# Two transformer blocks on one core: another order at the start of the mixers, fewer splits on GpSimd, and a shifted side job in the first feed-forward layer

## The chip, the cores and the metric

The kernel runs on one core of a Trainium2 chip. The metric is the device time of one execution in microseconds (us); the kernel before has three such runs, and beside them one execution was profiled. The engines are named as in the profile: PE (TensorE, matmuls; PEld its weight loads), DVE (VectorE), ACT (ScalarE), POOL (GpSimd) and SP (SyncE, which here issues nearly all DMAs; SPq is its queue). Each engine runs its own list of instructions strictly in order.

## The reference, cut to what matters

```
def first_block(x, c, ...):                 # x (1, 256, 1024), two layers
    cond = silu(c)
    for l in range(2):
        mod = cond @ ada_w[l] + ada_b[l]    # nine vectors of 1024: shift, scale, gate of three sublayers
        h = rms_norm(x, norm_g[l, 0]) * (1 + scale0) + shift0
        x = x + 0.5 * gate0 * swiglu(h, ffn1_w13[l], ffn1_w2[l])       # "ffn1"
        h = rms_norm(x, norm_g[l, 1]) * (1 + scale1) + shift1
        p = split(h @ w_in[l] + b_in[l])
        y = concat(nsa(p.a, t5 bias tables), short_conv(p.b), gated_deltanet(causal_conv4(p.c)), mlstm(p.d))
        x = x + gate1 * (y @ w_out[l])                                  # "mixer"
        x = x + 0.5 * gate2 * swiglu(adaln(x), ffn2_w13[l], ffn2_w2[l]) # "ffn2"
    return x
# second_block: LRU and latent attention, MLP, retention, MLP; the change does not touch it
```

All is float32. A product is made of three matmuls on rounded parts: each operand is split into `hi` (rounded) and `lo` (the rest), and hi·hi, hi·lo and lo·hi are summed in PSUM.

## The kernel before, in words

**Weights.** All weights lie in one HBM stream in the order of their use. `weights(key)` loads a chunk (128 partitions x 1024, 896 or 768 floats, 0.5 MB for 1024) with one DMA on the SP queue into a buffer `wraw` (4 buffers, L140); ACT copies it to `whi` (L150) and DVE, or POOL where the call passes `True`, subtracts to get `wlo` (L151). `whi` and `wlo` have 4 buffers each, so the loads can run 8 chunks ahead of PE. A 1024 chunk feeds 24 matmuls of 256 to 258 columns (L167, L168, L169).

**Order.** A scheduler that works with a timing model puts the instructions of each engine in order, from the program text and the priorities in it. `issue_after(last(SP))` ties a DMA to the one before it; while `in_order` is set (all of ffn1 of layer 0 up to w2) the SP queue keeps the order of the program text.

**ffn1 of layer 0** takes 0 to 245 us. The function `begin` does the first feature tiles (m = 0 to 7) with the normalisation still open, because the conditioning vectors `mod` are still being computed: a conditioning step loads a 0.5 MB chunk of `ada_w` into `wada` (3 buffers), multiplies it with `cond` and sums on DVE (L233, "a conditioning pass"). Of the 32 passes that go with this layer's scale, gate and shift vectors, `next(more)` in `begin` calls 4, the loop over m = 8 to 21 one per m, and the loop of the second product (w2, eight output tiles m with three chunks each) up to two per m. `begin` also computes `shift0` on PE by thin matmuls ("strips"), whose weights go through `wada` too. The loop over m ends each m with the gate: DVE multiplies by `rstd` (L384), ACT applies silu, DVE forms `sb` (L392), ACT and POOL split it into `g`.

**The side job** builds the relative-position bias tables. From m = SIDE = 12 on, each m calls `next(sides)` once: the loads of `ident`, `cst`, `tab` and `onehot` and four matmuls `st<-onehot,tab` (L474) with four copies `bv<-st` on ACT (L475) come first, then at the next m the store of `bv` to a DRAM scratch `bdram` (L484, on the SP queue), two m later the skewed load `bt<-bdram` (L487), and later the copies to `bc` (L494).

**A mixer** (layer 0: 245 to 456 us, layer 1: 846 to 1060 us) begins with six products of the gated-deltanet inputs (chunks `wc`, on un-normalised input) and one of scalars (`wsc`), all with their `wlo` split on POOL. `inputs()` then evacuates them: for each of six tiles DVE multiplies PSUM by `rstd` (`cxp`, L591) and adds a bias column (`cb`, L592), ACT adds the bias (L593), and DVE does the four taps of the causal convolution (`cx`, L595 and three times L597) with a sigmoid gate (L603). In its midst `scalars()` (L699 to L707) makes `scT` on DVE and transposes it on PE (L705). `norm()` makes the normed input `h` for the other products: `nt` (L349, DVE), `hhi` (L352, ACT), `hlo` (L353, DVE), eight tiles of each. Then come the product of `wa_3`, the token-major product `wta` in `proj_tok` (L733 to L735), the compression (L1180 on), and the rest. `weave` interleaves these generators by the numbers in `PACE`.

## Time and profile before

| | us |
|---|---|
| runs (three) | 1990.77, 1995.83, 1999.63; median 1995.83 |
| profiled execution, its own time | 2000.48 |
| its span in the trace | 1998.6 |
| PE busy in the span | 1926.8 |
| DVE, ACT, POOL busy | 1501.9, 1009.7, 566.0 |

Times in the trace count from the span's start. PEclk is the granted TensorE clock as a share of full speed; over the whole span it is 0.975. An instruction's duration overlaps the next one's a little on DVE, so starts lie closer than durations.

### The profile page before, as it was taken

The numbers are of one execution on the slowest core, as the hardware profiler recorded it, in microseconds if no ns is written. First come the engines' busy times: TensorE is split into PE (matmuls) and PEld (weight loads), VectorE is DVE, ScalarE is ACT, GpSimd is POOL, SyncE is SP. The second block draws the span as 40 slices with busy tenths as digits, with TensorE's granted clock in tenths as the row PEclk, the third lists the DMA queues.
The fourth block names the chain that finished last, engine by engine and source line by source line (L and its number), as shares of the span: only waits on it lengthen the run. The fifth ranks groups of instructions, "written<-read, shape, count | busy, mean of one in ns | idle before, by whom it ended". The sixth has DMA issues, their size and how long they took to land.

```text
span 1998.6 us, 40143 instructions
## 1 busy us (share of the span) xinstructions
PE 1926.8 (96%) x16031; PEld 1827.9 (91%) x16031; DVE 1501.9 (75%) x2693; ACT 1009.7 (51%) x1712; POOL 566.0 (28%) x474
## 2 busy tenths in 40 slices
...
GB/s 332 271 218 316 209 131 261 109 87 240 286 279 259 264 287 280 304 142 176 63 35 210 221 189 194 142 80 136 159 190 166 194 131 156 150 158 195 174 202 95
DMA packets 108808, 384.21 MB, mean 192 GB/s; under 512 B 12075, under 2 KB 14668, under 8 KB 108364
## 3 DMA queue, kind: packets, MB, share of 16 engines
...
## 4 chain that ended last, share of the span: by engine, by line
PE 85%; DVE 7%; DMA 3%; issue 2%; ACT 1%; POOL 1%; SPq 0%; POOLq 0%; ACTq 0%; DVEq 0%
PE acc L167 23%; PE acc L169 23%; PE acc L168 23%; DMA wraw<-in_stream_dram 2%; DVE wlo L151 1%; PE b L2007 1%; DVE wada L233 1%; PE pa L1284 1%; ACT whi L150 1%; PE pc L924 1%; PE pa L1311 1%; DVE vlo L292 1%; DMA g<-in_stream_dram 1%; PE pc L942 1%; PE acc L733 1%
## 5 line engine op out<-in xcount | busy, mean ns | idle before, releaser
L150 ACT ACTIVATE whi<-wraw 128x1024 fp32r<-128x1024 f32 (+2 forms) x546 | 563.5, 1036 | 466.3 <-PE acc L168 323.9
L151 DVE TENSOR_TENSOR wlo<-wraw,whi 128x1024 fp32r<-128x1024 f32 (+1 forms) x471 | 594.9, 1266 | 204.1 <-ACT whi L150 197.5
L167 PE MATMUL acc<-vhi,whi 128*128 128x258 f32 (+3 forms) x2176 | 621.7, 288 | 21.2 <-ACT whi L150 17.6
L168 PE MATMUL acc<-vlo,whi 128*128 128x258 f32 (+3 forms) x2176 | 620.8, 286 | 2.4 <-DVE vlo L292 2.4
L169 PE MATMUL acc<-vhi,wlo 128*128 128x258 f32 (+3 forms) x2176 | 615.6, 286 | 3.1 <-DVE wlo L151 3.0
L167 PEld LDWEIGHTS acc<-vhi,whi 128*128 128x128 f32 x2176 | 413.1, 191 | 28.9 <-ACT whi L150 19.5
L168 PEld LDWEIGHTS acc<-vlo,whi 128*128 128x128 f32 x2176 | 416.0, 191 | 5.3 <-DVE vlo L292 3.2
L169 PEld LDWEIGHTS acc<-vhi,wlo 128*128 128x128 f32 x2176 | 411.6, 190 | 6.9 <-DVE wlo L151 4.0
L151 POOL TENSOR_TENSOR wlo<-wraw,whi 128x1024 fp32r<-128x1024 f32 (+1 forms) x75 | 190.2, 2540 | 271.2 <-ACT whi L150 261.3
L168 PE MATMUL acc<-g,whi 128*128 128x256 f32 x704 | 199.2, 283 | 0.8 <-POOL g L151 0.8
L167 PE MATMUL acc<-g,whi 128*128 128x256 f32 x704 | 198.4, 282 | 1.3 <-ACT g L150 1.3
L169 PE MATMUL acc<-g,wlo 128*128 128x256 f32 x704 | 199.1, 283 | 0.0
L167 PE MATMUL acc<-hhi,whi 128*128 128x256 f32 (+1 forms) x576 | 169.7, 298 | 6.4 <-ACT whi L150 2.8
L169 PE MATMUL acc<-hhi,wlo 128*128 128x256 f32 (+1 forms) x576 | 168.7, 295 | 0.0
L168 PE MATMUL acc<-hlo,whi 128*128 128x256 f32 (+1 forms) x576 | 168.3, 293 | 0.0
L151 POOL TENSOR_TENSOR g<-sb,g 128x256 fp32r<-128x256 f32 x88 | 106.1, 1209 | 161.7 <-ACT g L150 150.5
L167 PE MATMUL acc<-ghi,whi 128*128 128x272 f32 (+1 forms) x512 | 146.4, 286 | 0.0
L169 PE MATMUL acc<-ghi,wlo 128*128 128x272 f32 (+1 forms) x512 | 145.9, 285 | 0.0
L168 PE MATMUL acc<-glo,whi 128*128 128x272 f32 (+1 forms) x512 | 145.7, 285 | 0.0
L167 PEld LDWEIGHTS acc<-g,whi 128*128 128x128 f32 x704 | 133.5, 190 | 1.5 <-ACT g L150 1.5
L168 PEld LDWEIGHTS acc<-g,whi 128*128 128x128 f32 x704 | 133.1, 189 | 1.0 <-POOL g L151 1.0
L169 PEld LDWEIGHTS acc<-g,wlo 128*128 128x128 f32 x704 | 133.2, 189 | 0.0
...
## 6 DMA issues: line engine op xcount, KB each, us to landing
...
wada<-in_stream_dram SPq DMA_DIRECT2D x128, 512.0 KB, 4.7
...
```

The lines of the kernel that those rows point to most:

```text
L150: self.nc.scalar.activation(hi, src, AF.Copy)
L151: (self.nc.gpsimd if pool else self.nc.vector).tensor_tensor(lo, src, hi.bitcast(F32), op=ALU.subtract)
L167: nc.tensor.matmul(ps, wh[:, kw], xh, start=start, stop=False)
L168: nc.tensor.matmul(ps, wh[:, kw], xl, start=False, stop=False)
L169: nc.tensor.matmul(ps, wl[:, kw], xh, start=False, stop=stop)
L233: nc.vector.scalar_tensor_tensor(w, w, 1.0, self.cond, op0=ALU.mult, op1=ALU.mult, accum_out=c)
L292: nc.vector.scalar_tensor_tensor(lo[:, m, 0:T], self.x[m], A[:, m:m + 1], hi[:, m, 0:T].bitcast(F32), op0=ALU.mult, op1=ALU.subtract)
L733: nc.tensor.matmul(ps[t], hh[:, tk], wh[:, kw], start=k == 0, stop=False)
L924: nc.tensor.matmul(ps[s, hh], M[s, t, hh], c["eye"][s] if v == 1 else de[t][s, 0, hh], start=True, stop=True)
L942: nc.tensor.matmul(ps[s, 1, hh], p1[t][s, hh], de[t][s, 1, hh], start=True, stop=True)
L1284: nc.tensor.matmul(ps[:, 0:n], qn[z, hh // 2, t * P:(t + 1) * P], keys[b, hh % 2][:, 0:n], start=True, stop=True)
L1311: nc.tensor.matmul(ps[:, hh], PT[hh][:, kb], v[:, kb, b], start=kb == 0, stop=kb == t)
```

## The change

In the mixers: nine of the twelve early `wlo` splits go from POOL to DVE (four of 128x1024, the 128x224 one, four of 128x768); POOL keeps the two of `a == 1` and the first of `a == 0`. `inputs()` now evacuates all six tiles first, one pair per turn; the convolutions are a function `conv(a)` called between the later products; the bias add `cb` and the first tap go to ACT; `scalars()` comes after the product of `wa_3`; the pace of `norm` is earlier. In gated deltanet and mLSTM four matmuls of a group are reordered.

In ffn1 of layer 0: SIDE is 9 instead of 12 with three more turns before the store, so the table loads and their four matmuls come three m earlier and the store stays at m = 13, the load `bt` comes at m = 14 instead of 15, the copies `bc` one later. The four passes of `begin` go to the w2 loop, which calls 18 (two per m, three at m = 2 and 5), each tied behind the last DVE instruction of the program text. The strips of `shift0` load into `wraw`.

```diff
--- before.py
+++ after.py
@@ -29,7 +29,7 @@
 WIDE = 6
 FIRST = 8
 PLACES = 16
-SIDE = 12
+SIDE = 9
 W2_CUTS = ((0, 8), (8, 15), (15, 22))
 
 
@@ -230,7 +230,8 @@
             for m in range(8):
                 w = self.raw(f"ada{l}_{j}_{m}", pool, name, bufs)
                 c, b = t[:, m:m + 1], self.cols[:, o + m:o + m + 1]
-                nc.vector.scalar_tensor_tensor(w, w, 1.0, self.cond, op0=ALU.mult, op1=ALU.mult, accum_out=c)
+                with self.tc.issue_after(self.last(mybir.EngineType.DVE)) if self.in_parts else ExitStack():
+                    nc.vector.scalar_tensor_tensor(w, w, 1.0, self.cond, op0=ALU.mult, op1=ALU.mult, accum_out=c)
                 if kind == 1:
                     g = self.col(f"g{l}_{s}")
                     if m == 0:
@@ -400,7 +401,7 @@
                 m0 = FIRST
                 self.in_order = True
                 steps = self.ada_parts(hp, ada1 + ada2)
-                late, extra = begin(psum, hp, steps)
+                late, extra = begin(psum, hp)
                 self.in_parts = True
                 sides = side(psum, hp)
             else:
@@ -441,13 +442,11 @@
             self.h = [(a[:, 0:TN], b[:, 0:TN]) for a, b in zip(*([v[:, k] for k in range(KD)] for v in (self.vhi, self.vlo)))]
             for m in range(KD):
                 ps = psum.tile([P, T], F32, name="acc2", bufs=3)
-                if begin:
-                    for _ in range(2):
+                for _ in () if begin else ada2:
+                    next(steps)
+                for k0, k1 in W2_CUTS:
+                    if begin and (k0 or m in (2, 5)):
                         next(steps, None)
-                else:
-                    for _ in ada2:
-                        next(steps)
-                for k0, k1 in W2_CUTS:
                     w = self.weights(f"w2_{l}_{s}_{m}_{k0}")
                     for k in range(k0, k1):
                         self.mm(ps, w, g[k], slice((k - k0) * P, (k - k0 + 1) * P), k == 0, k == FT - 1)
@@ -483,11 +482,10 @@
         d = dr.tile([P, 4, 384], F32, name="bdram")
         nc.sync.dma_start(d, self.bv)
         yield
-        yield
         nc.sync.dma_start(self.bt, bass.AP(tensor=d.tensor, offset=d.offset + 127, ap=[[1535, P], [384, 4], [1, T]]))
         nc.gpsimd.memset(self.bc, NEG)
-        yield
-        yield
+        for _ in range(4):
+            yield
         for t in range(2):
             n = 7 if t == 0 else 15
             o = 31 + 128 * (1 - t)
@@ -509,10 +507,10 @@
                     self.early_products([self.weights(k, True) for k in keys], ps, psum.tile([P, T], F32, name="pc"))
                 else:
                     for f in range(2):
-                        self.product(ps[f], self.weights(keys[f], True), self.u)
+                        self.product(ps[f], self.weights(keys[f], a == f == 0), self.u)
                 if a == 0:
                     self.early_ps[3] = self.product(psum.tile([28, T + 2], F32, name="pc", bufs=2),
-                                                    self.weights(f"wsc_{l}", True), self.u, 28)
+                                                    self.weights(f"wsc_{l}"), self.u, 28)
             self.weave([(self.inputs(), 0.0, 1.0), (self.gdn(), *PACE[l]["gdn"]),
                         (self.gates_mlstm(), *PACE[l]["mlstm"]), (self.conv(), *PACE[l]["conv"]),
                         (self.nsa(), *PACE[l]["nsa"]),
@@ -579,35 +577,37 @@
         nc, l = self.nc, self.l
         bF = lambda j: self.col(f"bF{l}", j)
         self.cx = [None] * 3
+        xps = [None] * 3
+
         for a in (1, 0, 2):
-            cv = self.cx[a] = self.t([P, 2, T], f"cx{a}")
-            xps = self.d2([P, 2, 3 + T], "cxp")
+            xps[a] = self.d2([P, 2, 3 + T], "cxp")
             for f in range(2):
-                j = 2 * a + f
-                xp = xps[:, f]
+                xp, ps = xps[a][:, f], self.early_ps[a][f]
                 nc.gpsimd.memset(xp[:, 0:3], 0.0)
-                ps = self.early_ps[a][f]
                 b = self.mx.tile([P, 1], F32, name="cb", bufs=2)
                 nc.vector.tensor_tensor(xp[:, 3:], ps[:, 0:T], self.rstd, op=ALU.mult)
-                nc.vector.tensor_tensor(b, ps[:, T:T + 1], bF(4 + j), op=ALU.add)
+                nc.scalar.activation(b, ps[:, T:T + 1], AF.Identity, bias=bF(4 + 2 * a + f))
                 nc.scalar.activation(xp[:, 3:], xp[:, 3:], AF.Identity, bias=b)
-                w = lambda i: self.col(f"gcw{l}", 4 * j + i)
-                nc.vector.tensor_scalar(cv[:, f], xp[:, 0:T], w(0), None, op0=ALU.mult)
+            yield
+
+        def conv(a):
+            cv = self.cx[a] = self.t([P, 2, T], f"cx{a}")
+            for f in range(2):
+                xp = xps[a][:, f]
+                w = lambda i: self.col(f"gcw{l}", 4 * (2 * a + f) + i)
+                nc.scalar.activation(cv[:, f], xp[:, 0:T], AF.Copy, scale=w(0))
                 for i in range(1, 4):
                     nc.vector.scalar_tensor_tensor(cv[:, f], xp[:, i:i + T], w(i), cv[:, f],
                                                    op0=ALU.mult, op1=ALU.add)
-                if f == 0:
-                    yield
             e = self.mx.tile([P, 2, T], F32, name="sg", bufs=2)
             self.sigmoid(e, cv)
             nc.vector.tensor_tensor(cv, cv, e, op=ALU.mult)
             self.ready.add(f"c{'qkv'[a]}")
-            yield
-            if a == 1:
-                self.scalars()
-                yield
+
         yield "h"
-        ps = self.proj(f"wa_{l}_3", True)
+        conv(1)
+        yield
+        ps = self.proj(f"wa_{l}_3")
         self.ak2 = []
         for b in range(2):
             s = slice(64 * b, 64 * b + 64)
@@ -616,11 +616,15 @@
             nc.scalar.activation(k2[64:128, 0:T - 1], ps[s, 1:T], AF.Identity, bias=bF(3)[s])
             self.ak2.append(k2)
         yield
+        self.scalars()
+        yield
+        conv(0)
+        yield
         self.av = self.t([P, 2, 2, 64], "av")
         v1 = self.t([P, 2, 4, 65], "dv1")
         nc.gpsimd.memset(v1[:, :, :, 64:65], 1.0)
         ps = [self.psum.tile([P, 384], F32, name="acc", bufs=2) for _ in range(2)]
-        yield from self.proj_tok([f"wta_{l}_{k}" for k in range(0, KD, 2)], ps, True)
+        yield from self.proj_tok([f"wta_{l}_{k}" for k in range(0, KD, 2)], ps, lambda: conv(2))
         bav, bdv = self.row(f"bav{l}"), self.row(f"bdv{l}")
         for t in range(2):
             nc.vector.tensor_tensor(v1[:, t, :, 0:64], ps[t][:, 128:].rearrange("p (h d) -> p h d", h=4),
@@ -718,13 +722,17 @@
         ps = self.psum.tile([P, T], F32, name="acc", bufs=2)
         return self.product(ps, self.weights(key, pool), self.h)
 
-    def proj_tok(self, keys, ps, pool=False):
+    def proj_tok(self, keys, ps, between=None):
+
 
         nc = self.nc
         n = ps[0].shape[-1]
         k = 0
         for key in keys:
-            wh, wl = self.weights(key, pool)
+            if between and k == KD // 2:
+                between()
+                yield
+            wh, wl = self.weights(key)
             for o in range(0, wh.shape[1], n):
                 hh, hl = self.h[k]
                 kw = slice(o, o + n)
...
@@ -1354,9 +1365,9 @@
             self.split(yb[:, f], *self.y_tile(2 + f))
 
 
-PACE = [{"gdn": (3.1, 0.64), "mlstm": (30.0, 1.5), "nsa": (30.0, 0.71), "norm": (0.5, 0.2), "ada": (22.0, 1.4),
+PACE = [{"gdn": (3.1, 0.64), "mlstm": (30.0, 1.5), "nsa": (30.0, 0.71), "norm": (0.1, 0.22), "ada": (22.0, 1.4),
          "out": (0.0, 2.0), "conv": (0.0, 1.0)},
-        {"gdn": (4.0, 0.7), "mlstm": (28.6, 1.23), "nsa": (30.0, 0.53), "norm": (0.5, 0.3), "ada": (30.0, 1.5),
+        {"gdn": (4.0, 0.7), "mlstm": (28.6, 1.23), "nsa": (30.0, 0.53), "norm": (0.1, 0.22), "ada": (30.0, 1.5),
          "out": (5.0, 0.5), "conv": (0.0, 1.0)}]
 
 OUT_ORDER = (2, 3, 6, 7, 0, 1, 4, 5)
@@ -2217,7 +2228,7 @@
         b.open1(ctx)
         dr = ctx.enter_context(tc.tile_pool(name="bd", bufs=1, space=DRAM))
 
-        def begin(psum, pool, more):
+        def begin(psum, pool):
 
             b.condition(c_ap)
             steps = b.ada_parts(pool, [(0, 1)])
@@ -2254,7 +2265,7 @@
 
                 if q == 0:
                     sums[h] = psum.tile([P, 2, 256], F32, name="st")
-                w = b.raw(f"ada0_0_{4 * h + q}", pool, "wada", 3)
+                w = b.raw(f"ada0_0_{4 * h + q}", b.wp, "wraw", WRAW)
                 a = [w[:, k % 4 * 256:(k % 4 + 1) * 256] for k in range(KD)]
                 b.strips(sums[h][:, q // 2], cond, a, range(4 * (q % 2), 4 * (q % 2) + 4))
 
@@ -2294,7 +2305,6 @@
                     ps = psum.tile([P, T], F32, name="acc")
                     b.product(ps, b.weights(f"w13_0_0_{m}_{z}", False, raws[-1]), [(a[:, 0:T], c[:, 0:T]) for a, c in b.u])
                     nc.vector.tensor_tensor(t[:, z], ps, b.rstd, op=ALU.mult)
-                    next(more)
                     if m == WIDE and z == 0:
                         finish(0)
                     for q in ((0,), (1,), (2, 3), ())[2 * (m - WIDE) + z]:
@@ -2337,7 +2347,8 @@
             nc.sync.dma_start(b.ident, b.ident_ap)
             b.constants1(cst_ap, where)
             b.bias_tables(t5_ap, onehot_ap, psum, pool)
-            yield
+            for _ in range(4):
+                yield
             yield from b.skew(dr)
 
         for l in range(2):
```

On the SP queue, around the tables and the scratch store in the loop over m of ffn1; a triple is one `wada` and two `wraw` loads, those of one m. Before:

```order
49 L468 DMA tab<-in_t_dram 32x4
50 L470 DMA onehot<-in_onehot_dram 33x384
51 L140 DMA wada<-in_stream_dram 128x1024
52 L140 DMA wraw<-in_stream_dram 128x1024 x2
53 L484 DMA bdram<-bv 128x1536
54 L140 DMA wada<-in_stream_dram 128x1024
55 L140 DMA wraw<-in_stream_dram 128x1024 x2
56 L140 DMA wada<-in_stream_dram 128x1024
57 L140 DMA wraw<-in_stream_dram 128x1024 x2
58 L487 DMA bt<-bdram 128x4x256
```

And with the change:

```order
44 L467 DMA tab<-in_t_dram 32x4
45 L469 DMA onehot<-in_onehot_dram 33x384
46 L140 DMA wada<-in_stream_dram 128x1024
47 L140 DMA wraw<-in_stream_dram 128x1024 x2
48 L140 DMA wada<-in_stream_dram 128x1024
49 L140 DMA wraw<-in_stream_dram 128x1024 x2
50 L140 DMA wada<-in_stream_dram 128x1024
51 L140 DMA wraw<-in_stream_dram 128x1024 x2
52 L140 DMA wada<-in_stream_dram 128x1024
53 L140 DMA wraw<-in_stream_dram 128x1024 x2
54 L483 DMA bdram<-bv 128x1536
```

Between the loads of the tables and the store that waits for `bv` lay one triple, and now there are four; from the store to the load of `bt` there were two triples, and now there is one.

On PE, where the last early product of mixer 0 ends (`acc<-vhi,whi` is still the un-normalised input, `acc<-hhi` the product of `wa_3`). Before:

```order
1740 L167 MATMUL acc<-vhi,whi 128x258
1741 L168 MATMUL acc<-vlo,whi 128x258
1742 L169 MATMUL acc<-vhi,wlo 128x258
1743 L705 MATMUL pc<-ident,scT 128x28 x2
1744 L167 MATMUL acc<-hhi_3083,whi 128x256
1745 L168 MATMUL acc<-hlo_3084,whi 128x256
1746 L169 MATMUL acc<-hhi_3083,wlo 128x256
```

And with the change:

```order
1742 L167 MATMUL acc<-vhi,whi 128x258
1743 L168 MATMUL acc<-vlo,whi 128x258
1744 L169 MATMUL acc<-vhi,wlo 128x258
1745 L167 MATMUL acc<-hhi_3083,whi 128x256
1746 L168 MATMUL acc<-hlo_3084,whi 128x256
1747 L169 MATMUL acc<-hhi_3083,wlo 128x256
```

The transpose of `scT` stood between the early products and `wa_3`; it now comes later, after 18 matmuls of the token-major product.

On DVE at the same place, from the scalars up to the evacuations whose PSUM bank `wa_3` takes (`cxp<-acc`; its last reader before is L592 in row 280). Before:

```order
270 L699 TENSOR_TENSOR scT<-pc,rstd 28x256
271 L701 COPY sb<-pc 28x1
272 L595 TENSOR_SCALAR cx_3153<-cxp,cols 128x256
273 L597 SCALAR_TENSOR_TENSOR cx_3070<-cxp,cols,cx_3070 128x256
274 L353 SCALAR_TENSOR_TENSOR hlo_3134<-nt,mod_3_1969,hhi_3133 128x256
275 L597 SCALAR_TENSOR_TENSOR cx_3153<-cxp,cols,cx_3153 128x256
276 L353 SCALAR_TENSOR_TENSOR hlo_3140<-nt,mod_3_1969,hhi_3139 128x256
277 L702 TENSOR_SCALAR scT<-scT,sb 28x256
278 L591 TENSOR_TENSOR cxp<-acc,rstd 128x256
279 L597 SCALAR_TENSOR_TENSOR cx_3153<-cxp,cols,cx_3153 128x256
280 L592 TENSOR_TENSOR cb<-acc,cols 128x1
281 L597 SCALAR_TENSOR_TENSOR cx_3153<-cxp,cols,cx_3153 128x256 x2
```

And with the change, where L588 is the evacuation, L600 a tap, L703 to L706 the scalars, L350 and L354 the `nt` and `hlo` of `norm`:

```order
266 L350 SCALAR_TENSOR_TENSOR nt<-z_77,mod_4_891,rstd 128x256
267 L350 SCALAR_TENSOR_TENSOR nt<-z_78,mod_4_891,rstd 128x256
268 L151 TENSOR_TENSOR wlo<-wraw,whi 128x768
269 L600 SCALAR_TENSOR_TENSOR cx_3220<-cxp,cols,cx_3220 128x256
270 L600 SCALAR_TENSOR_TENSOR cx_3151<-cxp,cols,cx_3151 128x256 x2
271 L588 TENSOR_TENSOR cxp<-acc,rstd 128x256
272 L706 TENSOR_SCALAR scT<-scT,sb 28x256
273 L151 TENSOR_TENSOR wlo<-wraw,whi 128x768
274 L600 SCALAR_TENSOR_TENSOR cx_3220<-cxp,cols,cx_3220 128x256
275 L354 SCALAR_TENSOR_TENSOR hlo_3131<-nt,mod_3_2164,hhi_3130 128x256
276 L354 SCALAR_TENSOR_TENSOR hlo_3137<-nt,mod_3_2164,hhi_3136 128x256
277 L588 TENSOR_TENSOR cxp<-acc,rstd 128x256
```

The splits of 128x768 now stand in this row, the first taps (L595) and the `cb` adds (L592) are gone from it, and `scT` no longer holds the product of `wa_3`. L588 in row 271 now frees the bank. From the first `nt` up to and with it the changed row holds 8 `nt`, 6 `hlo`, 5 evacuations, 8 taps, 5 splits (224, three of 1024, one of 768) and 2 small ones of the scalars.

## Rows read from the trace of the kernel before

**Rows 1.** The page, part 1 (busy us, share, instructions), DMA line.

```profile
PE 1926.8 (96%) x16031; PEld 1827.9 (91%) x16031; DVE 1501.9 (75%) x2693; ACT 1009.7 (51%) x1712; POOL 566.0 (28%) x474
...
DMA packets 108808, 384.21 MB, mean 192 GB/s; under 512 B 12075, under 2 KB 14668, under 8 KB 108364
```

**Rows 2.** Waits of PE, 0 to 245 us: us in total, times, longest.

```profile
PE acc L167 <- ACT whi L150: 17.6, 3, 10.4
PE acc L167 <- ACT g L150: 1.3, 1, 1.3
```

**Rows 3.** Waits of PE, 245 to 340 us.

```profile
PE pa L1213 <- issue: 5.1, 1, 5.1
...
PE pc L705 <- DVE scT L702: 5.0, 1, 5.0
...
PE acc L167 <- DVE cb L592: 2.2, 3, 1.8
```

**Rows 4.** Waits of PE over the whole span (layer 0 and layer 1).

```profile
PE pc L705 <- DVE scT L702: 10.0, 2, 5.0
```

**Rows 5.** Windows of 20 us: length, engines' busy us, PEclk, DMA share, GB/s.

```profile
120.00:140.00 20.00, 13.86 (x94) 12.81 (x94) 13.04 (x21) 8.66 (x15) 3.80 (x3) 0.83 0.91 345
140.00:160.00 20.00, 20.00 (x170) 20.00 (x169) 19.94 (x29) 10.63 (x21) 14.57 (x7) 1.00 0.88 325
180.00:200.00 20.00, 17.90 (x135) 17.49 (x134) 19.37 (x35) 11.38 (x18) 3.14 (x3) 0.91 0.95 344
260.00:280.00 20.00, 12.82 (x81) 12.04 (x80) 20.00 (x46) 10.55 (x20) 10.57 (x4) 0.75 0.39 119
```

**Rows 6.** Windows of 5 us, the same columns.

```profile
125.00:130.00 5.00, 0.62 (x2) 0.50 (x2) 2.44 (x5) 2.31 (x4) 1.40 (x2) 0.68 1.02 412
275.00:280.00 5.00, 5.00 (x25) 5.00 (x24) 5.00 (x15) 1.94 (x6) 0.98 (x1) 0.50 0.68 213
```

**Rows 7.** Timeline of the SP queue: start us, us, queue, line, transfer.

```profile
92.39 6.54 SPq L140 DMA_DIRECT2D wraw<-in_stream_dram  x2
...
121.43 0.33 SPq L484 DMA_DIRECT2D bdram<-bv  x1
```

**Rows 8.** Timeline of ACT: start us, us, instruction, [idle before <-releaser].

```profile
120.91 0.49 ACT L475 ACTIVATE bv<-st 128x384 f32<-128x384 f32 x1
...
128.27 1.06 ACT L150 ACTIVATE whi<-wraw 128x1024 fp32r<-128x1024 f32 x1 [2.47 <-DMA wraw<-in_stream_dram]
```

**Rows 9.** Timeline of DVE around the last gates of ffn1.

```profile
184.66 1.22 DVE L151 TENSOR_TENSOR wlo<-wraw,whi 128x1024 fp32r<-128x1024 f32 x1
...
185.80 0.47 DVE L392 SCALAR_TENSOR_TENSOR sb<-se,sh 128x256 f32<-128x256 f32 x1
...
186.27 1.21 DVE L233 SCALAR_TENSOR_TENSOR wada<-wada,cond 128x1024 f32<-128x1024 f32 x1
```

**Rows 10.** Groups of DVE, 245 to 290 us: xcount | busy us, mean ns.

```profile
L597 DVE SCALAR_TENSOR_TENSOR cx<-cxp,cols,cx 128x256 f32<-128x256 f32 x18 | 11.0, 629 | 0.0
L349 DVE SCALAR_TENSOR_TENSOR nt<-z,mod,rstd 128x256 f32<-128x256 f32 x8 | 7.8, 991 | 0.6 <-ACT rstd L326 0.6
L353 DVE SCALAR_TENSOR_TENSOR hlo<-nt,mod,hhi 128x256 fp32r<-128x256 f32 x8 | 6.8, 860 | 0.0
```

**Rows 11.** Timeline of POOL at the start of mixer 0.

```profile
262.99 4.89 POOL L151 TENSOR_TENSOR wlo<-wraw,whi 128x1024 fp32r<-128x1024 f32 x2 [3.97 <-ACT whi L150]
```

**Rows 12.** Timeline of DVE at the start of mixer 0.

```profile
252.12 1.69 DVE L349 SCALAR_TENSOR_TENSOR nt<-z,mod,rstd 128x256 f32<-128x256 f32 x3 [0.64 <-ACT rstd L326]
...
261.34 0.47 DVE L597 SCALAR_TENSOR_TENSOR cx<-cxp,cols,cx 128x256 f32<-128x256 f32 x1
...
263.98 2.21 DVE L353 SCALAR_TENSOR_TENSOR hlo<-nt,mod,hhi 128x256 fp32r<-128x256 f32 x1
```

**Rows 13.** Timeline of PE at the start of mixer 0.

```profile
274.51 0.55 PE L167 MATMUL acc<-hhi,whi 128*128 128x256 f32 x1 [1.80 <-DVE cb L592]
...
292.85 0.40 PE L796 MATMUL pd<-gl,cst 128*128 128x16 f32 x2
```

9 lines of the change are left out of this document (6 added, 3 removed).

## The prediction

> **What bounds the kernel now.** I read the page first: PE is busy 1926.8 us of a span of 1998.6, DVE 75%, ACT 51%, POOL 28%; the DMA engines moved 192 GB/s on the mean [rows 1]. So the kernel goes at PE's pace, and a change can give back only where PE stands still or runs at a lower clock. A list of PE's waits stage by stage finds those places, and the windows say what each is worth. A window of dense product work holds 170 matmuls in 20 us at a granted clock of 1.00, which is 0.118 us each [rows 5]; I count what a stretch lost by the matmuls that it falls short of that.
>
> *In ffn1 of layer 0*, PE waits three times for a weight chunk's `whi`, 17.6 us in all, and once for a gate's `g`, 1.3 us [rows 2]. Of the three, 10.4 us is the start of the kernel, which the change leaves alone. The large one that it touches lies in 120 to 140 us: 94 matmuls instead of 170, so (170 - 94) x 0.118 = 9.0 us are lost, part as standstill and part at a clock of 0.83 for the window [rows 5]. Its cause is on the SP queue. After the `wraw` loads that end at 98.9 us it issues nothing until 121.43, when it stores `bv` to `bdram`; the last copy into `bv` ends on ACT at 121.40 [rows 7, 8]. The reader is to see a store that waits for its data while all weight loads are queued behind it. The next chunk lands only at 128.27, where ACT ends a wait for a DMA with its copy [rows 8]; from 125 to 130 us PE does 2 matmuls, while the DMA engines now carry 412 GB/s [rows 6].
>
> The `g` wait is in 180 to 200 us, which holds 135 matmuls, 35 x 0.118 = 4.1 us short [rows 5]. There DVE is the late engine: 19.94 of 20 us in 140:160 and 19.37 in 180:200 [rows 5]. The `sb` of a last gate is made at 185.80, right behind a split and with a conditioning pass next [rows 9].
>
> *At the start of each mixer* PE waits 5.0 us for `scT` before the transpose, then again, 1.8 us for a `cb`, before the product of `wa_3` [rows 3, 4]. In 260 to 280 us PE is busy 12.82 us while DVE is busy all 20 [rows 5]. And when PE comes back its clock is 0.50: 25 matmuls in 5.00 us instead of 2.95, another 2.05 us [rows 6]. DVE is late partly because of its own work and partly because it is held: `hlo` at 263.98 lasts 2.21 us while a POOL split runs from 262.99, against 0.47 for an undisturbed instruction of that size [rows 11, 12]. Over this mixer's start the means of L597, L349 and L353 are 629, 991 and 860 ns [rows 10]; against 0.47 that is 18 x 0.16 + 8 x 0.52 + 8 x 0.39 = 10 us held.
>
> **The change part by part.** *The store.* `bv`'s matmuls and copies move three m up while the store stays at m = 13. One m is 48 matmuls, 48 x 0.118 = 5.7 us, so `bv` is ready some 17 us earlier against its store. The queue stood still from 98.9 to 121.4, which is 22.5 us; of that about 22.5 - 17 = 5.5 is left. The loads run 8 chunks ahead of PE, 8 x 24 x 0.118 = 22.7 us, so a hold of 5.5 us is covered and one of 22.5 us plus the landing is not. I take the whole 9.0 us, with 4 as the lower bound (if the four matmuls slip back towards the store). If the cover were gone, the old 9.0 is what it costs again. The load of `bt` one m earlier waits for a short store and is hidden in the same way.
>
> *Conditioning passes.* In DVE's order 25 passes stood ahead of the first output of w2 and 18 do now: 7 x 1.21 = 8.5 us [rows 9] of DVE work less ahead of the last gates. The gate that PE waits for was late by the 1.3 us of [rows 2] and what followed, so I take 3.5 of the 4.1 us; bounds 0 and 4.1. These passes come back in w2: 18 in eight m. One m there is 66 matmuls, 7.8 us of PE. DVE then has three splits of at most 1.22 (starts 1.14 apart in [rows 9]), 2.25 passes of about 1.3 with their small companions, and two of 0.47: 3.4 + 2.9 + 0.9 = 7.2 us. That fits, with 8% to spare. The loads fit as well: 18 x 0.52 MB and 8 x 1.44 MB (from chunk sizes) are 21 MB in 62.7 us, 335 GB/s, where 345 was seen for 20 us and 412 for 5 [rows 5, 6]. I cost it at 0, with up to 3 us lost as the bound.
>
> *The begin part.* Four passes and their 2 MB leave it, and the strips' chunks pass through `wraw`, where they take turns with weights. The trace of before has no such turn. The nearest rows bound it: the gain is at most the four passes, 4.8 us, the loss one wait like that of 120 to 140 us, 9. I take 0, since the loads leave room and the strips hold a buffer only for eight thin matmuls.
>
> *The mixer's chain.* What frees `wa_3` is the evacuation L588 in row 271 of DVE's new order. I walk DVE from the first `nt` at 252.12 [rows 12]. Durations overlap by 0.08 (1.22 against starts 1.14 apart, [rows 9]), so an instruction of 0.47 costs 0.40, an evacuation about 0.33. The row holds 8 `nt`, 6 `hlo` and 8 taps, 22 x 0.40 = 8.8; 5 evacuations, 1.65; splits 3 x 1.14 + 0.87 + 0.30, the last two scaled by size, 4.6; scalars 0.4. Together 15.45 us, to 267.6; ACT's small step follows, so `wa_3` starts at about 268.1 instead of 274.51 [rows 13]: **6.4 us**. The moved splits cost DVE more than nothing, but the walk has no POOL split beside it that holds it, since nine of twelve are gone. With plain durations instead the sum is 17.7 and the gain 4.2, the lower bound. `scT` is no longer in the chain; the transpose comes amid the token product, which has its own PE work around it.
>
> PE's last early product ends at about 267, or 266.4 without its small waits. So the gap shrinks from 6.8 to under 2 us, and the slow clock after it (2.05 us) is wholly or in part avoided. Gain per mixer: 6.4 with the same slow clock, 8.45 with none; I take 8.0. As L796, the start of the serial chain, came 18.3 us after `wa_3` [rows 13], and PE's own work fills that, the chain starts as much earlier. Mixer 1 shows the same wait, 10.0 us for the two together [rows 4]: 8.0 again. Both: 16, bounds 8 and 20.
>
> The first taps and `cb` on ACT (six each) cost it less than a 1.06 us split copy apiece [rows 8], and it is at 10.55 of 20 us [rows 5]: 0. The reordered matmuls in gated deltanet and mLSTM are as many as before: 0.
>
> *Sum.* 9.0 + 3.5 + 0 + 16 = 28.5 us. The profiled execution took 2000.48, so 1972; it lies 4.65 above the median of the three runs, so the median should go to 1995.83 - 28.5 = **1967**.
>
> **The rivals.** *(a) The mixers trade evenly.* DVE takes nine splits, 4 x 1.14 + 4 x 0.87 + 0.30 = 8.3 us, for about 10 us that it was held. Against it: five, not nine, of them stand ahead of `wa_3`, and the transpose no longer stands before it. Then only ffn1 pays, 12.5 us: **1983**. The page "Perfetto Trace Analysis" of the Trainium skill (section "Optimizing Scalar/DVE Operations") says that because GpSimd and DVE share an SBUF port, moving work between the two might not help; that rule stands for this rival. The trace agrees that they hold each other up (2.21 against 0.47 us above), which is why a DVE that runs alone can also come out ahead.
>
> *(b) ffn1 gives its gain back.* The 18 passes, tied behind the splits of their m, make `wlo` late in w2, or the begin part stumbles over `wraw`; 12.5 us go again. For it: only 8% of spare DVE time. Then the mixers alone pay: **1980**.
>
> *(c) The chain further on eats it.* PE waits 5.1 us before L1213 later in mixer 0 [rows 3]. If that chain is bound by POOL and DVE work that did not move, each mixer keeps only its slow clock and part of the gap, say 3 us: 12.5 + 6, **1977**.
>
> *(d) Slower.* In w2 a pinned pass that waits for its `wada` load holds up the splits queued behind it on DVE, and PE starves. If the queue delivered only the kernel's mean of 192 GB/s [rows 1], the 21 MB would take 109 us instead of 62.7: +46.6 - 28.5 is 18 us slower, **2014**. It decides below 21 MB / (62.7 + 28.5) = 230 GB/s. Against it: 345 and 325 GB/s in ffn1 itself [rows 5].
>
> *(e) Nothing much*: both halves fail, within 10 us of before.
>
> **How the numbers follow.** Forecast, all parts within their bounds: 0.58. (a) 0.14, (b) 0.08, (c) 0.10, (d) 0.04, (e) 0.06. Half a per cent, 10 us, is about what a measurement of this kernel can tell from no change, as its three runs lie 9 us apart. Faster by more: 0.58 + 0.14 + 0.08 + 0.10 less a margin of 0.02, 0.88; within: 0.07; slower: 0.05. The terms at their bounds all at once (4 to 9, 0 to 4.1, -3 to 0, -9 to 4.8, 8 to 20) would be 1958 to 1996; half of each distance, since they rarely fall on one side together, gives the forecast's own range, 1963 to 1982. The range that holds 8 in 10 takes in (a), (b) and (c), and at its lower end 1958 less the 4 us that single runs lie off their median: 1954 to 1985.
>
> **What would show it.** In the changed profile the SP queue should have no hole over 10 us before the store, the window at the place of 120 to 140 us should hold about 170 matmuls at clock 1.00, and no wait for `g` should stand before w2. `wa_3` should start some 16 us after the first `nt` (22.4 before), with a PE gap under 2 us ahead of it, and L597, L349 and L353 should be near 0.47 us. I am wrong if PE waits for `wlo` in w2, if DVE is still full from `nt` to `wa_3` for over 20 us, or if the gain is there at L796 and gone by the dense products behind it.

## The result and the profile after

| | before | after |
|---|---|---|
| median of runs (four each), us | 1996.37 | 1964.0 |
| span of the profiled execution, us | 1998.6 | 1966.5 |
| mean granted clock in it | 0.975 | 0.983 |

The ratio is 0.9846, 95% interval 0.9825 to 0.9866: 30.7 us faster (26.8 to 34.9), where the sum said 28.5 and a median of 1967. (The measurement gives this ratio itself; it is not quite the quotient of the two medians, which lie 32.4 us apart. All gains below go by such ratios.) The experiments show that the agreement is luck: two terms of the sum were wrong by about as much in opposite directions.

The page of the changed kernel, part 1 (as in [rows 1]: busy us, share, instructions):

```profile
PE 1909.4 (97%) x16031; PEld 1814.0 (92%) x16031; DVE 1489.7 (76%) x2687; ACT 1016.2 (52%) x1736; POOL 523.2 (27%) x456
```

PE has the same 16031 matmuls as in [rows 1] and is busy 17.4 us less. So of the 32.1 us by which the span is shorter, 14.7 are waits that went away and 17.4 are matmuls that take less time. The prediction priced PE's waits and one slow stretch behind them; only some of the 17.4 can be its slow clock.

*ffn1.* Waits of PE from 0 to 240 us (total, times, longest), against [rows 2]:

```profile
PE acc L167 <- ACT whi L150: 10.2, 1, 10.2
PE acc L167 <- ACT g L150: 1.4, 1, 1.4
PE acc L168 <- DVE vlo L293: 0.4, 1, 0.4
PE acc L168 <- POOL g L151: 0.3, 1, 0.3
```

Only the start of the kernel is left of the three waits for `whi`; the one for `g` is still there. Windows of ffn1 and of the mixer's start (250:260), columns as in [rows 5]:

```profile
120.00:140.00 20.00, 20.00 (x169) 20.00 (x168) 17.51 (x26) 10.20 (x23) 13.18 (x9) 1.00 0.66 243
...
160.00:180.00 20.00, 18.27 (x150) 17.86 (x150) 18.36 (x29) 10.58 (x17) 5.38 (x4) 1.00 0.82 281
180.00:200.00 20.00, 20.00 (x169) 20.00 (x168) 19.62 (x36) 9.12 (x13) 1.67 (x2) 1.00 0.98 368
200.00:220.00 20.00, 20.00 (x169) 20.00 (x169) 20.00 (x35) 10.49 (x16) 1.74 (x3) 1.00 0.99 357
250.00:260.00 10.00, 8.37 (x66) 8.16 (x66) 10.00 (x24) 6.76 (x14) 0.00 (x0) 1.00 0.52 154
```

120 to 140 us holds 169 matmuls where [rows 5] has 94. The product of w2 begins at 166.9 us with the waits for `g`; from 180 us on it runs at full rate, although DVE is busy nearly all the time and the DMA engines carry 357 to 368 GB/s. The store of `bv`, on the SP queue, now comes at 104.51 (121.43 in [rows 7]), after a hole of 6.2 us instead of 22.5, with loads right behind it:

```profile
97.50 0.86 SPq L140 DMA_DIRECT2D wraw<-in_stream_dram  x2
104.51 0.33 SPq L483 DMA_DIRECT2D bdram<-bv  x1
106.60 0.33 SPq L140 DMA_DIRECT2D wada<-in_stream_dram  x1
```

*The start of mixer 0.* Waits of PE from 235 to 330 us, against [rows 3], and PE's timeline at the places of [rows 13]:

```profile
PE pa L1224 <- issue: 3.5, 1, 3.5
PE acc L167 <- ACT cb L589: 1.6, 1, 1.6
PE acc L167 <- DVE dkT L650: 1.4, 1, 1.4
```

```profile
255.33 0.39 PE L167 MATMUL acc<-hhi,whi 128*128 128x256 f32 x1 [1.63 <-ACT cb L589]
...
271.02 0.40 PE L804 MATMUL pd<-gl,cst 128*128 128x16 f32 x2
```

The first `nt` starts at 239.4, so `wa_3` (255.33) comes 15.9 us after it, where it was 22.4; no wait for `scT` stands in the list, and the gap before `wa_3` is 1.63 us. The chain's first matmul (L804, before L796) comes 31.6 us after the first `nt`, before 40.7. Groups of DVE there (236 to 275 us, against [rows 10]):

```profile
L600 DVE SCALAR_TENSOR_TENSOR cx<-cxp,cols,cx 128x256 f32<-128x256 f32 x18 | 7.8, 470 | 0.0
...
L354 DVE SCALAR_TENSOR_TENSOR hlo<-nt,mod,hhi 128x256 fp32r<-128x256 f32 x8 | 3.5, 479 | 0.0
L350 DVE SCALAR_TENSOR_TENSOR nt<-z,mod,rstd 128x256 f32<-128x256 f32 x8 | 3.4, 479 | 0.6 <-ACT rstd L327 0.6
```

All three are undisturbed, and the clock from 250 to 260 us is 1.00. Up to here the signs are as forecast, but for the wait for `g`, which still stands. But from there to the end of mixer 0 the gain shrinks, and in mixer 1 it grows at a place that the prediction did not look at.

**Where the time lies, by stage.** I cut each profiled execution at the same five events: the first `nt` of a mixer, the copy of the first cumulated gates (`cum`, on DVE, right behind L796), and the first step of `rstd` of the ffn2 after it. In brackets: what the granted clock took, the sum over windows of 5 us of (1 - PEclk) x 5.

| profiled execution (run) | ffn1, to nt 0 | nt 0 to cum 0 | cum 0 to ffn2 | to nt 1 | nt 1 to cum 1 | cum 1 to ffn2 | rest |
|---|---|---|---|---|---|---|---|
| before | 252.1 (8.5) | 41.4 (5.1) | 180.4 (10.3) | 378.8 | 41.1 (5.2) | 181.7 (12.0) | 923.1 (9.2) |
| before, again (4) | 249.7 (5.1) | 41.4 (5.2) | 182.2 (10.2) | 378.8 | 40.3 (5.1) | 175.3 (6.8) | 922.9 (7.9) |
| after | 239.4 (0) | 32.3 (0) | 187.0 (15.4) | 379.3 | 35.6 (3.4) | 170.4 (5.1) | 922.5 (8.9) |
| after, again (12) | 240.9 (1.7) | 32.6 (0) | 177.5 (8.6) | 378.9 | 33.1 (0) | 169.9 (3.4) | 920.8 (8.6) |
| ffn1's edits only (1) | 240.8 (1.7) | 40.5 (3.4) | 193.4 (18.7) | 378.8 | 40.9 (5.1) | 176.0 (6.9) | 921.9 (9.1) |
| mixers' edits and reorder (2) | 250.9 (6.8) | 32.3 (0) | 175.6 (6.8) | 378.8 | 35.8 (3.5) | 172.1 (5.1) | 916.5 (3.2) |
| reorder only (3) | 252.4 (8.6) | 40.3 (3.4) | 181.9 (15.4) | 379.0 | 41.0 (5.2) | 165.7 (1.7) | 922.1 (9.1) |
| all but the reorder (5) | 240.9 (1.8) | 32.6 (0) | 186.6 (11.9) | 379.2 | 34.7 (1.7) | 184.4 (13.7) | 921.5 (8.7) |
| of ffn1 only the side job (8) | 242.8 (1.7) | 32.4 (0) | 181.5 (10.2) | 379.2 | 33.1 (0) | 168.5 (3.4) | 922.1 (10.3) |
| nine splits on POOL (9) | 241.0 (1.7) | 39.2 (3.5) | 172.1 (6.8) | 378.6 | 39.6 (5.1) | 164.3 (1.7) | 920.8 (8.2) |
| nsa paced 0.65 (10) | 240.4 (0) | 32.3 (0) | 176.5 (6.9) | 379.3 | 34.7 (1.7) | 167.6 (5.1) | 920.6 (8.3) |
| mlstm paced 1.3 (11) | 242.2 (1.7) | 32.3 (0) | 179.4 (5.1) | 378.9 | 35.7 (3.4) | 166.2 (3.4) | 922.3 (10.2) |

The third and sixth columns differ by several us from one execution to the next of the same kernel (after: 187.0 and 177.5; before: 181.7 and 175.3), so no single cell there proves anything; the timed runs below decide.

### The profile page after: what moved, and what is told of

It is laid out like the page before. It is cut to its first block, busy times and chain, and to the rows that moved or that the text cites. A ratio compares the mean times of both kernels' runs of the same rounds, so it can differ in the third digit from the quotient of the medians.

```text
span 1966.5 us, 40131 instructions
## 1 busy us (share of the span) xinstructions
PE 1909.4 (97%) x16031; PEld 1814.0 (92%) x16031; DVE 1489.7 (76%) x2687; ACT 1016.2 (52%) x1736; POOL 523.2 (27%) x456
## 4 chain that ended last, share of the span: by engine, by line
PE 83%; DVE 8%; DMA 4%; issue 2%; ACT 2%; POOL 1%; POOLq 0%; SPq 0%; ACTq 0%; DVEq 0%
PE acc L167 23%; PE acc L169 23%; PE acc L168 23%; DMA wraw<-in_stream_dram 3%; DVE wlo L151 2%; ACT whi L150 1%; PE b L2018 1%; DVE sb L393 1%; PE pa L1295 1%; PE pc L932 1%; DMA wada<-in_stream_dram 1%; DVE wada L234 1%; PE acc L741 1%; DMA rows<-in_rows_dram 1%; PE s L1834 0%
## 5 line engine op out<-in xcount | busy, mean ns | idle before, releaser
L151 DVE TENSOR_TENSOR wlo<-wraw,whi 128x1024 fp32r<-128x1024 f32 (+1 forms) x489 | 612.0, 1255 | 204.3 <-ACT whi L150 198.1
L167 PE MATMUL acc<-vhi,whi 128*128 128x258 f32 (+3 forms) x2176 | 620.0, 287 | 11.5 <-ACT whi L150 10.2
L167 PEld LDWEIGHTS acc<-vhi,whi 128*128 128x128 f32 x2176 | 410.4, 189 | 18.1 <-ACT whi L150 10.2
L151 POOL TENSOR_TENSOR wlo<-wraw,whi 128x1024 fp32r<-128x1024 f32 x57 | 144.6, 2538 | 221.9 <-ACT whi L150 210.7
```

What stands on the lines that cost most here:

```text
L151: (self.nc.gpsimd if pool else self.nc.vector).tensor_tensor(lo, src, hi.bitcast(F32), op=ALU.subtract)
L167: nc.tensor.matmul(ps, wh[:, kw], xh, start=start, stop=False)
```

## The experiments

The theory after the result was that of the prediction: two starts (ffn1's, the mixers') are earlier, and what follows is as much earlier. The rivals: an early start is spent before the mixer ends, and the reorder of matmuls, priced at nothing, pays. Each ratio is to the kernel before, timed on the same chip; in us it is that share of the median of the kernel before.

**1. ffn1's edits alone, in the kernel before.**

```diff
-SIDE = 12
+SIDE = 9
...
-                late, extra = begin(psum, hp, steps)
+                late, extra = begin(psum, hp)
...
-                w = b.raw(f"ada0_0_{4 * h + q}", pool, "wada", 3)
+                w = b.raw(f"ada0_0_{4 * h + q}", b.wp, "wraw", WRAW)
...
+                    if begin and (k0 or m in (2, 5)):
+                        next(steps, None)
```

> Only the edits of layer 0's ffn1 (SIDE, the scratch store and its load, the conditioning passes, the strips' buffers); both mixers as before. Theory A (the two halves add, stage by stage): mixer 0 begins 12.8 us earlier, the time falls by 12 to 13 us, ratio about 0.9937. Rival (the ffn1 part only lets the mixer wait for something else): mixer 0's first nt is 12.8 us earlier, but less than 8 us is left at the end.

Measured: 1991.81 against 1993.11, ratio 0.9994 (0.9972 to 1.0016): 1.2 us (-3.2 to 5.6). Mixer 0 begins about 10 us earlier and ends no earlier. The windows of this kernel towards the end of mixer 0 (columns as in [rows 6]):

```profile
415.00:420.00 5.00, 5.00 (x39) 4.04 (x38) 1.81 (x8) 0.38 (x1) 0.00 (x0) 0.73 0.00 0
420.00:425.00 5.00, 5.00 (x24) 3.68 (x23) 1.50 (x5) 1.23 (x3) 0.00 (x0) 0.50 0.00 0
425.00:430.00 5.00, 5.00 (x31) 3.85 (x30) 1.49 (x6) 1.15 (x4) 0.00 (x0) 0.50 0.00 0
430.00:435.00 5.00, 5.00 (x30) 4.43 (x28) 1.99 (x6) 1.03 (x4) 0.73 (x1) 0.50 0.01 3
```

PE is shown busy throughout, at the lower of its two clock levels (1.2 GHz, PEclk 0.50). From `cum` to ffn2 this execution takes 193.4 us with 18.7 lost to the clock; the two of before take 180.4 and 182.2 with 10.3 and 10.2. The stretch at 0.50 lasts from 417.3 to 437.8 us, which is 10.2 us lost, about as much as the mixer began earlier. From 414.0 us to the fall PE alternates between two shapes of matmul, a pattern that runs 3 and 5 to 7 are about:

```profile
416.47 0.33 PE L979 MATMUL pc<-cS,cqd 128*64 128x64 f32 x2
416.73 0.32 PE L980 MATMUL pc<-cvn,csegi 64*64 64x64 f32 x2
```

**2. The mixers' edits with the reorder, ffn1 as before.** Against the changed kernel:

```diff
-SIDE = 9
+SIDE = 12
...
-                late, extra = begin(psum, hp)
+                late, extra = begin(psum, hp, steps)
...
-                w = b.raw(f"ada0_0_{4 * h + q}", b.wp, "wraw", WRAW)
+                w = b.raw(f"ada0_0_{4 * h + q}", pool, "wada", 3)
```

> Only the edits of the mixers, with the reordered matmuls of gated deltanet and mLSTM; ffn1 as before. Theory A: 16 to 19 us faster, ratio about 0.991, with mixer 1 giving nearly all of it as in the changed kernel (mixer 0 about 0, mixer 1 about 16) because the low-clock stretches in the light second half of a mixer go with the order of its instructions. Rival B (these stretches come and go from one execution to the next or with the time at which the mixer begins): the first nt to wa_3 is 6.4 us shorter in both mixers again, but the split of the rest over mixers 0 and 1 differs, and the total may be anything from 8 to 26.

Measured: 1964.71, ratio 0.9852 (0.9824 to 0.9879), 29.5 us (24.1 to 35.1). That is the whole gain of the change within the interval, without any of ffn1, and more than either expectation had (16 to 19, at most 26).

**3. The reorder alone, in the kernel before.** Both edits: in gated deltanet the four state matmuls of a group first, then the four others (the diff of run 6); in mLSTM all eight state matmuls, then all eight others (the diff of run 7).

> Only the reordered matmuls in gated deltanet and mLSTM, all else as before. Theory C (this reorder is what kept PE at full clock at the end of mixer 1): the stretch of 17 us at a granted clock of 0.50 there is gone and the time falls by about 10 us. Theory A or B: no change within 3 us.

Measured: 1977.74, ratio 0.9915 (0.9885 to 0.9944), 16.9 us (11.2 to 22.9). The term of 0 was wrong.

**4. The kernel before, once more**, for the spread of its stages (second line of the table).

> The kernel before, profiled once more. Theory A: the stretch at a granted clock of 0.50 at the end of mixer 1 (1014 to 1031 us of the first trace) is there again at the same instructions. Rival B: it is absent or elsewhere.

Measured: 1992.49, one run. The stretch at 0.50 late in mixer 1 is there again, from 1008.5 to 1018.8 us (1014.3 to 1031.4 in the first execution).

**5. The whole change without the reorder.** Against the changed kernel (mLSTM's part; gated deltanet's is the reverse of run 6):

```diff
-            for hh in range(4):
-                for q in range(2):
-                    s = slice(64 * q, 64 * q + 64)
```

> The whole change without the reordered matmuls of gated deltanet and mLSTM. Theory C (the reorder by itself is worth what it gave alone, 15 us, because it keeps PE dense enough at the end of a mixer to hold its full clock): about 1979, 15 us slower than the whole change. Rival (its gain was an accident of the old order around it): within 4 us of the whole change, 1960 to 1968.

Measured: 1974.25 against 1993.92, ratio 0.9904 (0.988 to 0.9928), 19.1 us (14.4 to 23.9). Taking the reorder out costs 0.9904 - 0.9846 = 0.0058, 11.6 us, which is neither the 15 of the one expectation nor the 4 at most of the other, but nearer the first.

**6. The reorder of gated deltanet alone, in the kernel before.**

```diff
+            for hh in range(4) if ck else ():
+                nc.tensor.matmul(ps[s, hh], qd[hh % 2][:, hh // 2, tk], S[:, hh // 2], start=hh == 0, stop=False)
             for hh in range(4):
-                if ck:
-                    nc.tensor.matmul(ps[s, hh], qd[hh % 2][:, hh // 2, tk], S[:, hh // 2], start=True, stop=False)
```

> Only the reorder in gated deltanet (the four products with the old state ahead of the four that wait for the new values). If this is the active half of the reorder: 1978 to 1980, mixer 1's end without the stretch at 0.50. Otherwise 1990 to 1996.

Measured: 1984.71, ratio 0.9947 (0.9924 to 0.9969), 10.6 us (6.2 to 15.2). In its profile the reordered matmuls keep PE busy 8.3 us where before had 16.6, and the stretch at 0.50 late in mixer 1 is still there (1011.0 to 1017.9 us). So this half pays without that stretch going away.

**7. The reorder of mLSTM alone, in the kernel before.**

```diff
                     nc.tensor.matmul(pa[s, hh], qT[hh % 2][:, hh // 2, tk], C[:, 2 * t + q, hh // 2],
                                      start=True, stop=True)
+            for hh in range(4):
+                for q in range(2):
+                    s = slice(64 * q, 64 * q + 64)
                     nc.tensor.matmul(pb[s, hh], sT[s, t, hh], v1[s, t, hh], start=True, stop=True)
```

> Only the reorder in mLSTM (the products with the state together, then those with the scores). If this is the active half: 1978 to 1980. Otherwise 1990 to 1996. If the two halves add: each about 7 us faster.

Measured: 1983.46, ratio 0.995 (0.9927 to 0.9974), 10.0 us (5.2 to 14.6). Each half gives about 10 us, so neither alone is the active one (the sum, 20.6, and run 3's 16.9 agree within their intervals). Why it pays is seen on PE at the end of mixer 1. First the timeline of the kernel before, then that of run 7 (start us, us, line, tiles, rows*columns of the weights, x count; each matmul of the source is two instructions here):

```profile
1009.50 0.40 PE L989 MATMUL pc<-cu,ckd 64*64 64x64 f32 x7
1009.83 0.33 PE L1141 MATMUL pd<-dC,dqT 128*64 128x65 f32 x2
1010.09 0.33 PE L1143 MATMUL pd<-dv,dsT 64*64 64x65 f32 x2
1010.34 0.33 PE L1141 MATMUL pd<-dC,dqT 128*64 128x65 f32 x2
1010.60 0.33 PE L1143 MATMUL pd<-dv,dsT 64*64 64x65 f32 x2
```

```profile
1012.23 0.69 PE L1141 MATMUL pd<-dC,dqT 128*64 128x65 f32 x16
1012.84 0.68 PE L1146 MATMUL pd<-dv,dsT 64*64 64x65 f32 x16
1013.46 0.44 PE L1300 MATMUL pa<-ident,ap 128*128 128x128 f32 x2
```

Alternating between 128*64 and 64*64, two matmuls start every 0.257 us, 0.129 each; in one run of a shape, sixteen take 0.61, 0.038 each. The page "TensorEngine Tiling (Array Packing)" of the Trainium skill (section "Key Properties") says that a change of tiling mode drains TensorE; these rows fit it, though a drain has no row of its own. The single starts in the traces show that two things are in the difference. In gated deltanet, where all of a group write the same half of the partitions, grouped matmuls start every 0.058 us (run 6, 424.753 to 425.104 us), so a change of shape costs about 0.257 - 2 x 0.058 = 0.14 us, an estimate. In mLSTM's grouped order neighbours write different halves (q = 0 and 1), and there two start within 0.007 us of each other, every 0.058 us: they also run side by side.

The groups of PE by form over the whole span say what the reordered matmuls cost, before and after (busy us, mean ns):

```profile
L982 PE MATMUL pc<-cvn,csegi 64*64 64x64 f32 x48 | 8.3, 257 | 0.0
L981 PE MATMUL pc<-cS,cqd 128*64 128x64 f32 x48 | 8.3, 258 | 0.0
L1143 PE MATMUL pd<-dv,dsT 64*64 64x65 f32 x64 | 6.6, 257 | 0.0
L1141 PE MATMUL pd<-dC,dqT 128*64 128x65 f32 x64 | 5.8, 257 | 0.0
```

```profile
L990 PE MATMUL pc<-cvn,csegi 64*64 64x64 f32 x48 | 4.0, 224 | 0.0
L988 PE MATMUL pc<-cS,cqd 128*64 128x64 f32 x48 | 3.9, 225 | 0.0
L1154 PE MATMUL pd<-dv,dsT 64*64 64x65 f32 x64 | 3.3, 224 | 0.0
L1149 PE MATMUL pd<-dC,dqT 128*64 128x65 f32 x64 | 3.1, 229 | 0.0
```

That is 29.0 us of busy time against 14.3: 14.7 less for the same 224 matmuls, and 17.4 is what PE's busy time lost in all. It is a difference of two executions and not a pure price, as some of these matmuls ran at the lower clock before (the longest takes 369 ns, the shortest 216). Behind the alternation, before and run 7 differ once more in the windows at the end of mixer 1; here the kernel before, then run 7:

```profile
1015.00:1020.00 5.00, 5.00 (x35) 3.47 (x33) 1.99 (x10) 1.49 (x4) 0.00 (x0) 0.50 0.00 0
1020.00:1025.00 5.00, 5.00 (x29) 3.97 (x28) 1.55 (x5) 1.32 (x3) 0.00 (x0) 0.50 0.02 5
```

```profile
1015.00:1020.00 5.00, 5.00 (x59) 3.91 (x57) 3.10 (x12) 2.69 (x7) 0.00 (x0) 1.00 0.24 96
1020.00:1025.00 5.00, 5.00 (x56) 4.65 (x54) 2.92 (x11) 1.93 (x6) 0.99 (x1) 1.00 0.00 0
```

PE stands nowhere in either; the granted clock fell to 0.50 after the alternating stretch and stayed at 1.00 after the grouped one. Such a stretch lies late in mixer 1 in all five profiled executions without mLSTM's reorder (before twice, runs 1, 5 and 6; 6.9 to 20.5 us long), each beginning during the alternating matmuls or within 1 us of them, and in none of the nine with it. In mixer 0, where the same matmuls alternate, only run 1 of these has one directly behind them.

**8. The whole change, but of ffn1's edits only the shift of the side job**; passes and strips as before. Against the changed kernel:

```diff
-                    if begin and (k0 or m in (2, 5)):
+                if begin:
+                    for _ in range(2):
...
-                w = b.raw(f"ada0_0_{4 * h + q}", b.wp, "wraw", WRAW)
+                w = b.raw(f"ada0_0_{4 * h + q}", pool, "wada", 3)
```

> The mixers' edits with the reorder, and of the ffn1 part only the earlier tables (SIDE 9, store and load as in the change); the passes and the strips as before. Mixer 0's instructions come in yet another order here. Theory D (an earlier start of mixer 0 is kept or lost by the order that the scheduler then gives its second half): mixer 0 starts about 9 us earlier than in the run with the mixers' edits alone, and the end lies anywhere from 9 us earlier (1955) to equal (1964), as the gaps and low-clock stretches of its second half show. Rival E (something else fixes the end of mixer 0, a load or a chain from ffn1): mixer 0 ends at the same time as with the mixers' edits alone, with PE waiting for that one thing.

Measured: 1960.18, ratio 0.983 (0.9805 to 0.9856). It can't be told from the whole change (0.9846), nor from run 2 without any of ffn1's edits (0.9852): moving passes and strips shows no gain in the total, and that of the side job isn't clear of the noise.

**9. The whole change with the nine splits back on POOL.**

```diff
-                        self.product(ps[f], self.weights(keys[f], a == f == 0), self.u)
+                        self.product(ps[f], self.weights(keys[f], True), self.u)
...
-        ps = self.proj(f"wa_{l}_3")
+        ps = self.proj(f"wa_{l}_3", True)
...
-            wh, wl = self.weights(key)
+            wh, wl = self.weights(key, n == 384)
```

> The whole change, but the nine early splits of each mixer stay on POOL; the new order of evacuations, convolutions and the transpose stays. Theory (the splits' move matters, since POOL's long splits hold DVE's instructions): the means of the nt, hlo and tap instructions rise again from 0.48 us towards 0.6 to 1.0, first nt to the cum copy is 36 to 38 us instead of 32.3, 4 to 6 us lost per mixer, about 1972. Rival (an even trade between POOL and DVE): within 1 us per mixer of the whole change.

Measured: 1958.97, ratio 0.9832 (0.9809 to 0.9855): no slower than the whole change (run 12, same chip, 0.9846), where the theory had 8 to 12 us. Its groups of DVE from 236 to 282 us, then its wait before `wa_3`:

```profile
L600 DVE SCALAR_TENSOR_TENSOR cx<-cxp,cols,cx 128x256 f32<-128x256 f32 x18 | 13.0, 751 | 0.3 <-ACT az L790 0.2
L354 DVE SCALAR_TENSOR_TENSOR hlo<-nt,mod,hhi 128x256 fp32r<-128x256 f32 x8 | 6.7, 858 | 0.0
L350 DVE SCALAR_TENSOR_TENSOR nt<-z,mod,rstd 128x256 f32<-128x256 f32 x8 | 6.2, 800 | 0.6 <-ACT rstd L327 0.6
```

```profile
PE acc L167 <- ACT cb L589: 5.6, 2, 4.9
```

So the splits on POOL do hold DVE (751, 858 and 800 ns instead of 470 to 479), PE waits 4.9 us again, and `cum` comes 39.2 us after `nt` instead of 32.6. None of it is seen in the total: in these executions cum to ffn2 is shorter by 5.4 and 5.6 us than in run 12.

**10 and 11. The whole change with another pace for one generator of mixer 0.** This changes the scheduler's order behind the start and nothing else. Here run 10; run 11 leaves "nsa" and makes "mlstm" (30.0, 1.3).

```diff
-PACE = [{"gdn": (3.1, 0.64), "mlstm": (30.0, 1.5), "nsa": (30.0, 0.71), "norm": (0.1, 0.22), "ada": (22.0, 1.4),
+PACE = [{"gdn": (3.1, 0.64), "mlstm": (30.0, 1.5), "nsa": (30.0, 0.65), "norm": (0.1, 0.22), "ada": (22.0, 1.4),
```

> The whole change with another pace for NSA in layer 0 (0.65 for 0.71): the scheduler then puts 25 product matmuls of other groups between the fourth and the fifth softmax transpose of mixer 0 instead of 8. Theory D (ffn1's 12 us were given back because PE waits there for the softmax and its clock then drops): no wait over 1 us at that transpose, no low-clock stretch behind it, and cum to the delta rule's state chain takes about 128 us instead of 139; 1953 to 1958. Rival F (the chain of softmaxes and inverses, not PE's order, sets that length): the wait moves to another place and the time stays at 1962 to 1966.

> The whole change with another pace for mLSTM in layer 0 (1.3 for 1.5), a second order of the same instructions in mixer 0 (15 product matmuls at the place where the change has 8). Theory D: the length of cum to state chain changes with the order, between 127 and 140 us, and the time with it, 1953 to 1966, without mixer 0's start moving. Rival F: 139 us and 1962 to 1966 again.

Measured: run 10 1952.13, ratio 0.9795 (0.9773 to 0.9817), 40.8 us (36.4 to 45.2); run 11 1954.35, 0.9813 (0.9791 to 0.9835), 37.2 us. Both are better than the change itself on the same chip (run 12, 0.9846); for run 10 the intervals lie apart (0.9817 and 0.9825), for run 11 they overlap. From `cum` to the delta rule's state chain (the first L980 of the mixer, `pc<-cS,cwT`) run 10 takes 127.7 us and run 11 131.7, where the changed kernel took 139.5 in its first profile. In that profile PE waits twice for the softmax tile `ap` in 330 to 400 us, and its clock falls behind the second wait (timeline, windows):

```profile
340.22 0.33 PE L1308 MATMUL pa<-ident,ap 128*128 128x128 f32 x1 [1.47 <-ACT ap L1300]
...
360.94 0.33 PE L1308 MATMUL pa<-ident,ap 128*128 128x128 f32 x1 [2.56 <-ACT ap L1300]
```

```profile
365.00:370.00 5.00, 5.00 (x61) 4.06 (x60) 1.45 (x6) 0.50 (x2) 0.00 (x0) 0.50 0.02 5
370.00:375.00 5.00, 5.00 (x39) 4.35 (x37) 1.54 (x5) 0.99 (x3) 0.00 (x0) 0.51 0.00 0
```

In run 10 no such wait is listed, and the same place runs at full clock:

```profile
350.00:360.00 10.00, 10.00 (x140) 8.70 (x138) 7.04 (x18) 3.14 (x9) 0.73 (x1) 1.00 0.48 151
360.00:370.00 10.00, 10.00 (x161) 9.06 (x161) 8.16 (x20) 2.59 (x7) 0.92 (x3) 1.00 0.37 118
```

What differs in front of the waiting transpose is product work: in the changed kernel PE has 8 product matmuls between the transposes at 352.06 and 360.94, in run 10 it has 25 between those at 348.07 and 355.42.

**12. The changed kernel, once more.**

> The changed kernel again, on the chip of these runs. Theory D (order): the wait at the fifth softmax transpose of mixer 0 and the low clock behind it are there again, cum to state chain 135 us or more; 1962 to 1966. Rival B (chance of one execution): they are gone.

Measured: 1960.94 against 1991.17, ratio 0.9846 (0.9825 to 0.9867), as at first. In this execution the second wait for `ap` is 0.43 us instead of 2.56 and the clock stays at 1.00 from 350 to 380 us; cum to the state chain takes 129.9 us, cum to ffn2 177.5 instead of 187.0 (timeline, then a window):

```profile
359.76 0.33 PE L1308 MATMUL pa<-ident,ap 128*128 128x128 f32 x1 [0.43 <-ACT ap L1300]
360.00:370.00 10.00, 10.00 (x160) 8.61 (x159) 6.65 (x21) 2.08 (x7) 0.00 (x0) 1.00 0.17 55
```

So the long slow stretch of the first profile belongs to that execution, not to every one of this kernel, and the theory that runs 10 and 11 cured it isn't borne out: rival B is. The execution profiled here was the fastest of its six (1955.54), and that of run 11 the slowest of its five (1958.7), so their stages are no measure of what separates the medians.

## Why the prediction was right, and where it was not

The time (1964.0 for 1967) and the sign came out, the time by luck: ffn1 gave some 11 us less than its term, the mixers some 3 less, and the reorder some 17 that stood at 0. By its steps:

- **The store, 9.0 us: right at its place.** 169 for 94 matmuls in the window is 75 x 0.118 = 8.9 us, and the cause (a store that waits for `bv`, with loads behind it) went as described.
- **The wait for `g`, 3.5 us: wrong size.** It is still 1.4 + 0.3 us and its window holds 150 matmuls, 20 x 0.118 = 2.4 us short where 4.1 had been: 1.7 gained. **The begin part, 0**: with 12.7 us by the first `nt` in this profile, 12.7 - 8.9 - 1.7 = 2.1 are left for it, within its bounds. Over the table's rows ffn1 ends at 240.6 on the mean with these edits and at 251.3 without: 10.7 us at that place, for 12.5.
- **The passes in w2, 0: right.** 169 matmuls in each window of 20 us, at 357 to 368 GB/s; rivals (b) by late splits and (d) are out.
- **"Starts earlier" taken as "ends earlier": this step failed for ffn1.** It stood in no term; every gain at a start was added to the end. Run 1 gives 1.2 us (-3.2 to 5.6) of the 12.5; the whole change less run 2 is 1.2 us as well. It is the last of the prediction's own signs of being wrong: the gain is there at L796 and gone behind it. The outcome is rival (b)'s (ffn1 gives its gain back), by a cause that the prediction did not have: not in w2 or `begin`, but later, between `cum` and the end of mixer 0, where the time is spent again (in run 1's profile with a slow stretch that takes 10.2 us; what takes it in the others is open, below).
- **The mixers, 16 us: right at the place, 12.6 in the total.** By the profiles nt to cum shrank by 9.1 and 5.5 us (8.8 and 8.0 in run 12) against the 8.0 each. By the ratios, run 2 less run 3 is 29.5 - 16.9 = 12.6 us, between the bounds of 8 and 20 (as a difference of two, its own interval is some 8 us to each side). But that the early start is what pays isn't shown: run 9 has 39.2 and 39.6 us for this stretch and is no slower. `wa_3` itself came 15.9 us after the first `nt`, where the walk of DVE had 16.0. The nine splits, which this walk needed, are worth nothing measurable in the total; rival (a) is right for them, though not by its mechanism, as DVE is freed and `wa_3` is earlier.
- **"As many as before: 0" for the reordered matmuls: this term failed most.** It is 16.9 us (11.2 to 22.9) in run 3, 11.6 by run 5. Counting matmuls was the error: the price of one depends on the shape of the one before it. It could have been read beforehand, in PE's timeline of the kernel before (run 7). There the alternation costs 0.129 a matmul, and seven of one shape start within 0.33 us (1009.50 to 1009.83), 0.047 each; 224 times 0.082 less would have been 18.4 us, an estimate of the most that it can give. 14.7 is what the busy time shows.

The parts add up: 1.2 for ffn1 and 29.5 for run 2 are 30.7, the measured gain. (The 12.6 is itself run 2 less run 3, so splitting the 29.5 proves nothing more.) They do not add up exactly everywhere: run 5 gave 19.1 for ffn1 and mixers, where 1.2 + 12.6 = 13.8 would be expected; the intervals cover it.

**What is open.** How far an earlier start of mixer 0 is kept may depend on the order behind it. Runs 10 and 11 start as early (240.4 and 242.2 us), with another order, and are 10.1 and 6.5 us better than the change by the ratios on the same chip. So the order behind the start is worth something of the size of what ffn1 lost. That ffn1's time was lost through this order is not shown: neither pace was tried without ffn1's edits, where it may gain as much. Which wait or which slow stretch takes the time in the median execution isn't settled either, because the stretches come and go between executions of one kernel. Nor is it settled which of the mixers' remaining edits (evacuations first, `scalars()` later, the pace of `norm`, `cb` on ACT) makes the 12.6 us. Whether mLSTM's reorder pays through the matmuls themselves or through the slow stretch that they left behind can't be split cleanly either: run 7's total (10.0) holds both, and its reordered matmuls are 5.3 us less busy than before (12.4 to 7.1).
